# The last normalisation of a decoder layer: sums on VectorE, an earlier third token tile, a shorter Newton step, and a gain vector scaled beforehand

## The chip, the cores and the metric

The kernel runs on one core of one Trainium2 chip. The metric is device microseconds of that core for one execution, from the start of the program to its end. It is given as the median of several executions, and one further execution is taken by the hardware profiler.

## The reference

One layer of a hybrid decoder, on x of 1 x 512 x 1024 in float32, everything in float32:

```
u = rms_norm(x, norm_mix_g)
z = u @ w_in                        # q, k, v of attention; q, k, v, gates of the mLSTM; branch gates
A = block-sparse causal attention (8 heads x 64, rotary, blocks of 256)
B = chunkwise mLSTM (4 heads x 128, running-max stabiliser)
h = x + (sigmoid(gA) * (A @ w_proj_a) + sigmoid(gB) * (B @ w_proj_b)) @ w_out
u = rms_norm(h, norm_ffn_g)
g, up = split(u @ w_gate_up)        # 2 x 2816 columns
h = h + (silu(g) * up) @ w_down
return rms_norm(h, norm_final_g)

def rms_norm(x, g):
    return x * rsqrt(mean(x * x, axis=-1) + 1e-6) * g
```

The change concerns the last line: for each of the 512 tokens the sum of squares of its 1024 values of h, a reciprocal square root, and the product with it and with the gain vector `norm_final_g`.

## The kernel before

**Precision.** A float32 matmul is done as three TensorE products of float32r parts: each operand is split into a high part (`act_` with Copy on ScalarE, recorded at L155) and a low part, operand minus high part (VectorE, L168 in the helper `split_hl`, L847 in `gc_prep` for the weights of gate and up). One operand split thus always goes ScalarE first, then VectorE, then TensorE.

**The feed-forward part.** It is most of the program's second half. It runs through a list `ITEMS`: chunks "gc" of gate and up, single tiles "gu" of what is left of them, and chunks "ds" of the down projection. Each item is one level of Strassen's scheme: seven products named W11, S1, S2, W12, S3, S4 and W22. For each product of the first chunk, weights are loaded as `raw`, copied to w on ScalarE, and subtracted to a low w on VectorE (L847); sums of weights are made in DRAM by accumulating DMAs, `ws`. The other operand, `bq`, comes from the mixer's output and is split in the same way (ScalarE L155, VectorE L168) while the first products run already. TensorE's products of the chunk are L872, L873 and L874; their results are evacuated as `ga`, `gx` and `gb` on ScalarE and added to later products on VectorE (`gx` at L908).

**The second norm** falls into the first chunk. The column sums of squares of h are split into `sqh` (ScalarE) and `sql` (VectorE), both are multiplied by a matrix of ones on TensorE (L349), and the reciprocal root is computed and sent by DMA through DRAM to a per-token layout, `rg`, which the scaling of `gx` (ScalarE, L160) reads.

**What sets the order.** The kernel is written against a scheduler that keeps a priority for each instruction. `plan()` gives every product of every item a planned time, and `at(key, w, off)` sets the priority of what follows to that time plus an offset. An instruction may be placed ahead of its planned time where the scheduler finds its engine free and its operands there; `tc.issue_after(i)` keeps one behind instruction i. What comes out is one fixed sequence for each engine, and each engine takes its sequence in order. DMAs are issued by SyncE (SP), GpSimd (POOL) and in one case ScalarE.

**The end.** `end_load` (L1327 to L1336), called after the last but one "gu" item, loads the two halves of the final gain vector, `g3[0]` and `g3[1]`, broadcast to 128 partitions (128 x 512 each, DMA of L1332 on SP), and later the residual h in eight tiles `hs[t][j]`: token tile t of 128 tokens, column half j of 512. The two g3 loads wait for no computed value; the scheduler puts them on SP in the middle of the program, during the first gate-and-up chunk. Nothing reads g3 until the end.

`ds_end` (L1185 to L1325) is the last down chunk together with the final norm. Its matmuls are `ds_prod` (L1117 to L1119) and `last` (L1235 to L1237). Behind them, per token tile t and half j:

- `add_` (L1201, VectorE): h += product * factor of the second norm;
- `square` (ScalarE): squares of a half, with their sum as a second output;
- `rstd` (L1213 to L1217): VectorE adds the first sum and the epsilon to z, ScalarE takes Ln(e + z) and Exp(-0.5 * ...), e being the last sum, and VectorE forms v = e + z;
- `newton` (L327 to L335): one Newton step on that root r in three VectorE instructions, t = r*r, t = -0.5*t*v, t = (t + 1.5)*r;
- `apply` (L1221 to L1224): one half as h * factor * g on VectorE, the other, which `times_g` (L1227) has multiplied by g before, as h * factor on ScalarE, and then two stores on SP (for the fourth tile one of them on ScalarE).

The fourth token tile (t = 3) is last. Its half j = 1 is done in two column halves of 256 (`lo`, `hi`), so that the very last addition and square are half as wide. The third tile's `apply(2, ...)` is pinned behind that last addition.

Of the kernel before, what the change touches and what calls it, by code (L numbers as in the profile page):

```python
# [11 lines left out]
AF = mybir.ActivationFunctionType  # L12
ALU = mybir.AluOpType
# [4 lines left out]
D = 1024  # L18
# [5 lines left out]
EPS = 1e-6  # L24
# [67 lines left out]
def hybrid_layer_kernel(ctx: ExitStack, tc, xT, wall, wgc, wgu, wds, wdl, g3v, vecs, wgates, consts, rope, out):  # L92
    nc = tc.nc
    V, A, T = nc.vector, nc.scalar, nc.tensor
# [11 lines left out]
    def nm(p="t"):  # L106
        cnt[0] += 1
        return f"{p}{cnt[0]}"

    def slot(dt=F32, name="a"):  # L110
        return act.tile([P, S], dt, name=nm(name), tag="A")
# [8 lines left out]
    def blk2(dt=F32, name="b", raw=False):  # L120
        return blk(dt, name, raw).rearrange("p (x c) -> p x c", x=2)
# [18 lines left out]
    raw_ins = lambda i: getattr(i, "ins", i)  # L140

    def table(set_id):
        if ph["set"] == set_id:
            return
        with ExitStack() as es:
            for i in ph["ins"]:
                es.enter_context(tc.issue_after(i))
            ld = A.add_instruction(
                mybir.InstLoadActFuncSet(name=nc.get_next_instruction_name(), act_func_set_id=set_id)
            )  # L150
        ph.update(set=set_id, load=raw_ins(ld), ins=[])

    def act_(out_, in_, func, **kw):
        if func not in SETS:
            return A.activation(out_, in_, func, **kw)  # L155
        table(SETS[func])
        if ph["manual"]:
            return A.activation(out_, in_, func, **kw)
        with tc.issue_after(ph["load"]):
            i = A.activation(out_, in_, func, **kw)  # L160
        ph["ins"].append(raw_ins(i))
        return i
# [66 lines left out]
    for k in range(KT):  # L229
        for j in (0, 2) if k == 0 else (0,):  # L230
            c = slice(j * P, (j + 2) * P if k == 0 else S)
# [51 lines left out]
    for k in range(KT):  # L283
        if k < 4:
            t = blk2(F32R, "u", raw=k < 2)
# [5 lines left out]
        c = slice(0, P * len(halves[0]))  # L291
# [10 lines left out]
        for js in halves:  # L302
            if js[0]:
                c = slice(2 * P, S)
# [14 lines left out]
    for i in range(4):  # L319
        z = zqk["qk"[i // 2], i % 2] = slot(name="z")  # L320
# [8 lines left out]
    def newton(r, v, new):  # L329

        t = new()
        V.tensor_tensor(t, r, r, op=ALU.mult)
        V.scalar_tensor_tensor(t, t, -0.5, v, op0=ALU.mult, op1=ALU.mult)
        V.scalar_tensor_tensor(t, t, 1.5, r, op0=ALU.add, op1=ALU.mult)
        return t  # L335
# [467 lines left out]
    def at(key, w, off=0):  # L803
        t = clock["at"][key, w] + off
        tc.cur_priority = clock["base"] + (t if t > 0 else t // PRE)
# [379 lines left out]
    def ds_end():  # L1185


        n = NG - 1
        key = ("ds", n)
        w = sw.pop(key)["w"]  # L1190
        r, nr = ([st[x][:, t : t + 1] for t in range(4)] for x in ("rc", "nrc"))
        two = range(2)
        g3, hs = st["h"]
        ss = {}
        U = 1360
        v_ = lambda: small([P, 1], "v1")

        def add_(t, j, ps, c, d=slice(0, S)):

            h = hs[t][j][:, d]  # L1200
            return V.scalar_tensor_tensor(h, ps[:, d], c, h, op0=ALU.mult, op1=ALU.add)  # L1201

        def square(t, j, d=slice(0, S)):
            s = v_()
            act_(slot(name="sq")[:, d], hs[t][j][:, d], AF.Square, scale=D**-0.5, accum_out=s)
            ss.setdefault(t, []).append(s)

        def rstd(t, w_, o):

            at(key, w_, o - 600)  # L1210
            *s, e = ss[t]
            z, v, q = v_(), v_(), v_()
            i = V.tensor_scalar(z, s[0], s[-1] if len(s) > 1 else 0.0, EPS, op0=ALU.add, op1=ALU.add)  # L1213
            at(key, w_, o)
            act_(q, e, AF.Ln, bias=z)
            V.tensor_tensor(v, e, z, op=ALU.add)
            return q, v, (i, act_(q, q, AF.Exp, scale=-0.5))  # L1217

        def apply(t, q, j):

            V.scalar_tensor_tensor(hs[t][j], hs[t][j], q, g3[j], op0=ALU.mult, op1=ALU.mult)  # L1221
            act_(hs[t][1 - j], hs[t][1 - j], AF.Copy, scale=q)
            for e in (j, 1 - j):
                (nc.scalar if t == 3 and e != j else nc.sync).dma_start(out[t][:, e * S : e * S + S], hs[t][e])  # L1224

        def times_g(t, j):
            V.tensor_tensor(hs[t][j], hs[t][j], g3[j], op=ALU.mult)  # L1227

        def last(ps, t, j, first=False, d=slice(0, S)):

            q, c = slice(t * P, (t + 1) * P), slice(j * S + d.start, j * S + d.stop)
            for k in range(LK):
                (ah, al), (wh, wl) = hid[k], DL[k]
                g = dict(skip_group_check=not first)
                T.matmul(ps[:, d], ah[:, q], wh[:, c], start=first and k == 0, stop=False, **g)  # L1235
                T.matmul(ps[:, d], ah[:, q], wl[:, c], start=False, stop=False, **g)
                T.matmul(ps[:, d], al[:, q], wh[:, c], start=False, stop=k == LK - 1, **g)  # L1237

        qs = []
        X, Z = [mmb() for t in two], [sb() for t in two]  # L1240
        for t in two:
            at(key, "W11", U * t)
            ds_prod(X[t], w["W11"], n, 0, t, first=True)
            at(key, "S2", U * t)
            add_(t, 0, X[t], nr[t])
        for t in two:
            at(key, "S1", U * t)
            ds_prod(Z[t], w["S1"], n, 1, t, first=True)
        for t in two:
            at(key, "S2", U * t)  # L1250
            ds_prod(X[t], w["S2"], n, 4, t)
            at(key, "W12", U * t)
            add_(t + 2, 0, X[t], nr[t + 2])
        for t in two:
            at(key, "W12", 2 * U * t)
            y = accb()
            last(y, t, 0, first=True)
            ds_prod(y, w["W12"], n, 2, t)
            at(key, "W12", 2 * U * (t + 1) + D_OFF)
            add_(t, 0, y, r[t])  # L1260
            square(t, 0)
        for t in two:
            at(key, "S3", U * t)
            ds_prod(X[t], w["S3"], n, 5, t)
            at(key, "S3", U * t + D_OFF)
            add_(t + 2, 1, X[t], r[t + 2])
        for t in two:
            at(key, "W22", U * t - 1000)
            add_(t + 2, 1, Z[t], r[t + 2])
        at(key, "LAST")  # L1270
        y = accb()
        last(y, 2, 1, first=True)
        at(key, "W22", 2000)
        add_(2, 1, y, nr[2])
        square(2, 1)
        for t in two:
            at(key, "W22", 2 * U * t)
            ds_prod(X[t], w["W22"], n, 6, t)
            last(X[t], t, 1)
            at(key, "W22", 2 * U * t + 1000)  # L1280
            times_g(t, 0)
            at(key, "W22", 2 * U * (t + 1) + 200)
            add_(t, 1, X[t], r[t])
            square(t, 1)
            q, v, _ = rstd(t, "W22", 2 * U * (t + 1) + 2000)
            qs.append(newton(q, v, v_))
            if t == 0:
                apply(0, qs[0], 1)
        at(key, "S4")
        ds_prod(Z[0], w["S4"], n, 3, 0)  # L1290
        last(Z[0], 2, 0)
        at(key, "S4", 1000)
        times_g(2, 1)
        at(key, "S4", 2 * U + 200)
        add_(2, 0, Z[0], nr[2])
        square(2, 0)
        q, v, i = rstd(2, "S4", 2 * U + 1000)
        qs.append(newton(q, v, v_))
        at(key, "S4", 2 * U + 800)
        with tc.issue_after(raw_ins(i[1])):  # L1300
            apply(1, qs[1], 1)
        y = accb()
        lo, hi = slice(0, HS), slice(HS, S)
        at(key, "S4", 2 * U)
        last(y, 3, 1, first=True, d=lo)
        at(key, "S4", 3 * U)
        add_(3, 1, y, nr[3], lo)
        square(3, 1, lo)
        at(key, "S4", 5 * U // 2)
        ds_prod(Z[1], w["S4"], n, 3, 1)  # L1310
        last(Z[1], 3, 0)
        at(key, "S4", 9 * U // 2 + 200)
        add_(3, 0, Z[1], nr[3])
        square(3, 0)
        at(key, "S4", 9 * U // 2)
        last(y, 3, 1, first=True, d=hi)
        at(key, "S4", 5 * U + 200)
        i = add_(3, 1, y, nr[3], hi)
        square(3, 1, hi)
        with tc.issue_after(raw_ins(i)):  # L1320
            apply(2, qs[2], 0)
        q, v, i = rstd(3, "S4", 5 * U + 800)
        with tc.issue_after(raw_ins(i[0])):
            times_g(3, 0)
        apply(3, newton(q, v, v_), 1)  # L1325

    def end_load():  # L1327

# [405 lines left out]
    while n < len(steps) or qa or qb:  # L1734
        if qa and (len(qa) >= LA or n >= len(steps)):
            kind, h, b, r = qa.pop(0)
            qb.append((kind, h, b, moba_b(h, b, r) if kind == "a" else r, n))
        if n < len(steps):
# [3 lines left out]
            r, second = moba_a(h, b) if kind == "a" else ml_a(h, b)  # L1742
# [23 lines left out]
        while qb and (qb[0][4] <= n - LC):  # L1766
            kind, h, b, r, _ = qb.pop(0)
# [120 lines left out]
```

## Time and profile before

| | before |
|---|---|
| median of three executions | 720.25 us (719.82 to 720.83) |
| profiled execution, own time | 719.12 us |
| its span, from first to last recorded work | 717.3 us |
| mean granted TensorE clock | 0.998 of full speed |
| instructions | 9566 |
| DMA | 152.70 MB, mean 213 GB/s |
| chain that ended last, by engine | PE 84%, DVE 7%, ACT 5%, DMA 2% |

Engines are named as in the profile: PE is TensorE's matmul, PEld its weight load, DVE VectorE, ACT ScalarE, POOL GpSimd, SP SyncE; SPq and POOLq are the DMA issues of those two. A row of the timeline gives start and busy time in us, the engine, the line, the operation, the output and the operands by the program's names, and the tile's shape; in square brackets stands how long the engine was idle before it and what ended that. A row of the table of DMAs ends with the KB of one transfer and the median time from issue to landing. A row of the windows gives the stretch, its length, the busy time of PE, PEld, DVE, ACT and POOL (with the number of instructions), the granted clock, the mean busy share of the 16 DMA engines, and GB/s.

### The profile page before, as it was taken

The numbers are of one execution on the slowest core, as the hardware profiler recorded it, in microseconds if no ns is written. First come the engines' busy times: TensorE is split into PE (matmuls) and PEld (weight loads), VectorE is DVE, ScalarE is ACT, GpSimd is POOL, SyncE is SP. The second block draws the span as 40 slices with busy tenths as digits, with TensorE's granted clock in tenths as the row PEclk, the third lists the DMA queues.
The fourth block names the chain that finished last, engine by engine and source line by source line (L and its number), as shares of the span: only waits on it lengthen the run. The fifth ranks groups of instructions, "written<-read, shape, count | busy, mean of one in ns | idle before, by whom it ended". The sixth has DMA issues, their size and how long they took to land.

```text
span 717.3 us, 9566 instructions
## 1 busy us (share of the span) xinstructions
PE 707.3 (99%) x3318; PEld 588.4 (82%) x3318; DVE 601.4 (84%) x982; ACT 428.9 (60%) x706; POOL 69.9 (10%) x97
## 2 busy tenths in 40 slices
PE   9999999999999999999999999999999999999995
PEld 6888788888888888888888888888888888888974
DVE  6899886898987588666699869898899799798996
ACT  7634778669774346732354845566765665665655
POOL 0013010000001000000020110011002004003000
PEclk9999999999999999999999999999999999999999
DMA  9668683625158998988889866579569649969703
GB/s 331 283 211 238 200 230 119 201 90 191 60 184 220 278 268 247 273 255 230 224 270 237 252 224 197 214 185 297 192 196 273 220 134 222 312 162 275 203 1 118
DMA packets 47008, 152.70 MB, mean 213 GB/s; under 512 B 5852, under 2 KB 6244, under 8 KB 42480
## 3 DMA queue, kind: packets, MB, share of 16 engines
q1 hardware_dynamic: 36880, 117.39, 47.7%
q0 software_dynamic: 9792, 34.14, 22.9%
q8 instruction: 26, 0.43, 0.2%
q10 hardware_dynamic: 288, 0.56, 0.2%
q14 instruction: 22, 0.18, 0.1%
HBM read 130.01 MB, written 53.52 MB: 256 GB/s over the span
## 4 chain that ended last, share of the span: by engine, by line
PE 84%; DVE 7%; ACT 5%; DMA 2%; issue 1%; POOL 0%; ACTq 0%; DVEq 0%; POOLq 0%
PE mm L208 10%; PE mm L209 10%; PE mm L210 10%; PE mm L872 5%; PE mm L873 5%; PE mm L874 5%; PE s L873 2%; PE s L874 2%; PE s L872 2%; PE mm L1118 2%; PE mm L1119 2%; PE mm L1117 2%; PE mm L491 2%; PE mm L308 2%; PE mm L493 2%; PE mm L492 2%
## 5 line engine op out<-in xcount | busy, mean ns | idle before, releaser
L155 ACT ACTIVATE w<-raw 128x1024 fp32r<-128x1024 f32 (+2 forms) x107 | 108.1, 1023 | 49.1 <-PE mm L873 14.7
L155 ACT ACTIVATE wh<-raw 128x1024 fp32r<-128x1024 f32 x56 | 59.1, 1056 | 73.0 <-PE mm L209 70.7
L847 DVE TENSOR_TENSOR w<-raw,w 128x1024 fp32r<-128x1024 f32 x70 | 84.1, 1219 | 15.7 <-ACT w L155 15.6
L168 DVE TENSOR_TENSOR wl<-raw,wh 128x1024 fp32r<-128x1024 f32 x56 | 68.2, 1219 | 10.5 <-ACT wh L155 10.0
L872 PE MATMUL mm<-w,bq 128*128 128x512 f32 x160 | 62.4, 390 | 0.0
L874 PE MATMUL mm<-w,bq 128*128 128x512 f32 x160 | 62.3, 389 | 0.0
L873 PE MATMUL mm<-w,bq 128*128 128x512 f32 x160 | 62.2, 389 | 0.0
L208 PE MATMUL mm<-u,wh 128*128 128x512 f32 x128 | 50.6, 395 | 0.2 <-ACT ob L155 0.2
L210 PE MATMUL mm<-u,wh 128*128 128x512 f32 x128 | 50.1, 391 | 0.0
L209 PE MATMUL mm<-u,wl 128*128 128x512 f32 x128 | 49.9, 390 | 0.0
L210 PE MATMUL mm<-ul,wh 128*128 128x512 f32 x128 | 49.8, 389 | 0.0
L208 PE MATMUL mm<-uh,wh 128*128 128x512 f32 x128 | 49.8, 389 | 0.0
L209 PE MATMUL mm<-uh,wl 128*128 128x512 f32 x128 | 49.8, 389 | 0.0
L872 PEld LDWEIGHTS mm<-w,bq 128*128 128x128 f32 x160 | 30.0, 188 | 6.7 <-ACT gs L160 0.5
L873 PEld LDWEIGHTS mm<-w,bq 128*128 128x128 f32 x160 | 30.1, 188 | 6.2
L874 PEld LDWEIGHTS mm<-w,bq 128*128 128x128 f32 x160 | 30.0, 188 | 6.2
L1027 DVE TENSOR_TENSOR w<-raw,w 128x1024 fp32r<-128x1024 f32 x25 | 30.2, 1216 | 2.0 <-ACT w L155 1.0
L1117 PE MATMUL mm<-w,ac 128*128 128x512 f32 x80 | 31.3, 392 | 0.0
L1118 PE MATMUL mm<-w,ac 128*128 128x512 f32 x80 | 31.1, 389 | 0.0
L1119 PE MATMUL mm<-w,ac 128*128 128x512 f32 x80 | 31.1, 389 | 0.0
L872 PE MATMUL s<-w,bq 128*128 128x512 f32 x80 | 31.1, 389 | 0.0
L873 PE MATMUL s<-w,bq 128*128 128x512 f32 x80 | 31.1, 389 | 0.0
(439 smaller groups left out, 1942.0 us busy)
## 6 DMA issues: line engine op xcount, KB each, us to landing
raw<-in_wall_dram SPq DMA_DIRECT2D x56, 512.0 KB, 5.5
raw<-in_wgc_dram SPq DMA_DIRECT2D x30, 512.0 KB, 6.1
raw<-ws SPq DMA_DIRECT2D x30, 512.0 KB, 5.9
ws<-in_wgc_dram SPq DMA_DIRECT2D x10, 1024.0 KB, 6.5
ws<-in_wgc_dram POOLq DMA_DIRECT2D x10, 1024.0 KB, 10.1
raw<-in_wds_dram SPq DMA_DIRECT2D x15, 512.0 KB, 6.0
ws<-in_wds_dram SPq DMA_DIRECT2D x10, 512.0 KB, 7.9
ws<-in_wds_dram POOLq DMA_DIRECT2D x10, 512.0 KB, 7.0
```

The source lines that it names most:

```text
L155: return A.activation(out_, in_, func, **kw)
L168: V.tensor_tensor(l, src, f(h), op=ALU.subtract)
L208: st["mm"] = T.matmul(ps, wh[:, c], rh[j], start=start and j == 0, stop=False)
L209: T.matmul(ps, wl[:, c], rh[j], start=False, stop=False)
L210: T.matmul(ps, wh[:, c], rl[j], start=False, stop=stop and j == n - 1)
L847: V.tensor_tensor(l, t, f(h), op=ALU.subtract)
L872: st["mm"] = T.matmul(ps[t], bh, wh[:, d], start=first and k == 0, stop=False, skip_group_check=not first)
L873: T.matmul(ps[t], bh, wl[:, d], start=False, stop=False, skip_group_check=not first)
L874: T.matmul(ps[t], bl, wh[:, d], start=False, stop=k == 3, skip_group_check=not first)
L1117: T.matmul(ps, bh, wh[:, d], start=first and k == 0, stop=False, skip_group_check=not first)
L1118: T.matmul(ps, bh, wl[:, d], start=False, stop=False, skip_group_check=not first)
L1119: T.matmul(ps, bl, wh[:, d], start=False, stop=k == 1, skip_group_check=not first)
```

## The change

It has four parts, all in `ds_end`.

1. Both halves of the gain vector are multiplied by -0.5 on ScalarE, in place, at the planned time of the chunk's first product.
2. `rstd` is split into `start` (z, Ln, Exp) and `finish`. With -0.5 in the gain, a Newton step takes two VectorE instructions instead of three: c = q*v*q and r = (c - 3)*q, which is -2 times the value of before. v = e + z stands in `finish`.
3. The third tile's Newton step and `apply(2, ...)` are chained behind `apply(1, ...)` and ahead of the addition of tile 3, half 0, where `apply(2, ...)` stood behind the last addition before. `apply(1, ...)` is now pinned behind the first quarter's addition of tile 3 as well.
4. The last squares (128 x 256 of tile 3) are summed on VectorE by one instruction that multiplies, scales by 1/1024 and sums, starting from z3 (the first square's sum plus the epsilon), where ScalarE squared before; the last square of half 0 enters as the bias of Ln. `times_g(3, 0)` is pinned behind v instead of z.

```diff
@@ ds_end
         g3, hs = st["h"]
+        at(key, "W11")
+        for g in g3:
+            act_(g, g, AF.Copy, scale=-0.5)
...
+            z, q = v_(), v_()
+            V.tensor_scalar(z, s[0], s[-1] if len(s) > 1 else 0.0, EPS, op0=ALU.add, op1=ALU.add)
             at(key, w_, o)
+            cs[t] = q, e, z
             act_(q, e, AF.Ln, bias=z)
+            return act_(q, q, AF.Exp, scale=-0.5)
+
+        def finish(t):
+
+            q, e, z = cs[t]
+            v, c, r = v_(), v_(), v_()
             V.tensor_tensor(v, e, z, op=ALU.add)
-            return q, v, (i, act_(q, q, AF.Exp, scale=-0.5))
+            V.scalar_tensor_tensor(c, q, v, q, op0=ALU.mult, op1=ALU.mult)
+            return r, V.scalar_tensor_tensor(r, c, -3.0, q, op0=ALU.add, op1=ALU.mult)
...
-        q, v, i = rstd(2, "S4", 2 * U + 1000)
-        qs.append(newton(q, v, v_))
-        at(key, "S4", 2 * U + 800)
-        with tc.issue_after(raw_ins(i[1])):
-            apply(1, qs[1], 1)
+        j2 = start(2, "S4", 2 * U + 1000)
...
         at(key, "S4", 3 * U)
-        add_(3, 1, y, nr[3], lo)
+        i = add_(3, 1, y, nr[3], lo)
         square(3, 1, lo)
+        at(key, "S4", 2 * U + 900)
+        with tc.issue_after(raw_ins(i)), tc.issue_after(raw_ins(j2)):
+            i = apply(1, qs[1], 1)
+        with tc.issue_after(raw_ins(i)):
+            rr = finish(2)
+        qs.append(rr[0])
+        with tc.issue_after(raw_ins(rr[1])):
+            i = apply(2, qs[2], 0)
+        z3 = v_()
+        with tc.issue_after(raw_ins(i)):
+            V.tensor_scalar(z3, ss[3][0], EPS, None, op0=ALU.add)
...
-        add_(3, 0, Z[1], nr[3])
+        with tc.issue_after(raw_ins(i)):
+            add_(3, 0, Z[1], nr[3])
         square(3, 0)
         at(key, "S4", 9 * U // 2)
         last(y, 3, 1, first=True, d=hi)
         at(key, "S4", 5 * U + 200)
-        i = add_(3, 1, y, nr[3], hi)
-        square(3, 1, hi)
+        add_(3, 1, y, nr[3], hi)
+        e = v_()
+        i = V.tensor_tensor_reduce(
+            slot(name="sq")[:, hi], hs[3][1][:, hi], hs[3][1][:, hi], 1.0 / D, z3, op0=ALU.mult, op1=ALU.add, accum_out=e,
+        )
+        at(key, "S4", 5 * U + 800)
+        q, v, c, r = (v_() for _ in range(4))
+        act_(q, e, AF.Ln, bias=ss[3][1])
+        act_(q, q, AF.Exp, scale=-0.5)
+        i = V.tensor_tensor(v, e, ss[3][1], op=ALU.add)
         with tc.issue_after(raw_ins(i)):
-            apply(2, qs[2], 0)
-        q, v, i = rstd(3, "S4", 5 * U + 800)
-        with tc.issue_after(raw_ins(i[0])):
-            times_g(3, 0)
-        apply(3, newton(q, v, v_), 1)
+            i = times_g(3, 0)
+        with tc.issue_after(raw_ins(i)):
+            V.scalar_tensor_tensor(c, q, v, q, op0=ALU.mult, op1=ALU.mult)
+        V.scalar_tensor_tensor(r, c, -3.0, q, op0=ALU.add, op1=ALU.mult)
+        apply(3, r, 1)
```

The sequences of TensorE, GpSimd and SyncE are the same before and after, but for the order of the two stores of tiles 0 and 2. ScalarE has one instruction more, VectorE two fewer.

Where the two scalings of g3 stand is not where the code stands. The first is in ScalarE's sequence in the middle of the program, in the first gate-and-up chunk. In the names, the trailing numbers are buffers: g31317 is g3[0], w a weight's high part made from raw, bq the other operand's high part made from v1.

```order
 L155 ACTIVATE bq763_3689<-ut779_3781 128x512
 L155 ACTIVATE w795_3819<-raw767_3699 128x1024
+L155 ACTIVATE g31317_6274<-g31317_6274 128x512
 L155 ACTIVATE bq773_3737<-v1816_3889 128x512
 L155 ACTIVATE w797_3823<-raw768_3700 128x1024
```

One instruction is new, between the copy of a weight and the split of an operand; around it nothing is moved. The second, g31318 for g3[1], stands some twenty instructions further on in the same sequence, among the copies of weights.

```order
 L148 ACT_TABLE_LOAD
 L155 ACTIVATE w811_3853<-raw785_3797 128x1024
+L155 ACTIVATE g31318_6275<-g31318_6275 128x512
 L155 ACTIVATE w813_3857<-raw786_3798 128x1024
 L155 ACTIVATE w829_3925<-raw819_3905 128x1024
```

Again one row is added and none is moved. The last place is VectorE's end. Before, from the third tile's Newton step (L332 to L334) on; h11323 is tile 2 half 0, h11325 and h11326 are tile 3 halves 0 and 1, and the 128x1 tiles v1... are the sums and factors of one value per token:

```order
L332 TENSOR_TENSOR v11406_6701<-v11405_6696 128x1
L333 SCALAR_TENSOR_TENSOR v11406_6701<-v11406_6701,v11404_6695 128x1
L334 SCALAR_TENSOR_TENSOR v11406_6701<-v11406_6701,v11405_6696 128x1
L1201 SCALAR_TENSOR_TENSOR h11325_6282<-s1379_6514,nrc2_4096,h11325_6282 128x512
L1201 SCALAR_TENSOR_TENSOR h11326_6283<-acc1407_6709,nrc2_4096,h11326_6283 128x256
L1221 SCALAR_TENSOR_TENSOR h11323_6280<-h11323_6280,v11406_6701,g31317_6274 128x512
L1213 TENSOR_SCALAR v11414_6750<-v11408_6717,v11410_6733 128x1
L1227 TENSOR_TENSOR h11325_6282<-h11325_6282,g31317_6274 128x512
```

And the same stretch in the changed kernel, where L1235 and L1236 are the Newton step, L1240 is the third tile's scaling, L1204 are the additions and L1347 is the sum of squares:

```order
L1235 SCALAR_TENSOR_TENSOR v11411_6717<-v11406_6697,v11410_6716 128x1
L1236 SCALAR_TENSOR_TENSOR v11412_6718<-v11411_6717,v11406_6697 128x1
L1240 SCALAR_TENSOR_TENSOR h11323_6280<-h11323_6280,v11412_6718,g31317_6274 128x512
L1334 TENSOR_SCALAR v11413_6726<-v11408_6709 128x1
L1204 SCALAR_TENSOR_TENSOR h11325_6282<-s1379_6516,nrc2_4096,h11325_6282 128x512
L1204 SCALAR_TENSOR_TENSOR h11326_6283<-acc1407_6701,nrc2_4096,h11326_6283 128x256
L1347 ISA sq1417_6752,v11416_6751<-h11326_6283,v11413_6726 128x256
L1347 ISA v11416_6751 128x1
L1354 TENSOR_TENSOR v11419_6755<-v11416_6751,v11414_6741 128x1
L1247 TENSOR_TENSOR h11325_6282<-h11325_6282,g31317_6274 128x512
L1358 SCALAR_TENSOR_TENSOR v11420_6756<-v11418_6754,v11419_6755 128x1
L1359 SCALAR_TENSOR_TENSOR v11421_6757<-v11420_6756,v11418_6754 128x1
```

The third tile's scaling (h11323) has moved from behind both additions to ahead of them, the Newton step has one row fewer, and behind the second addition stands the sum of squares where before the third tile's scaling stood. On ScalarE the third tile's Exp now stands behind the half-wide square of tile 3 (sq1409), and the very last square has gone:

```order
L160 ACTIVATE v11406_6697<-v11403_6693,v11405_6696 128x1
L155 ACTIVATE sq1409_6710,v11408_6709<-h11326_6283 128x256
L160 ACTIVATE v11406_6697<-v11406_6697 128x1
L155 ACTIVATE h11321_6278<-h11321_6278,v11402_6675 128x512
L155 ACTIVATE h11324_6281<-h11324_6281,v11412_6718 128x512
L155 ACTIVATE sq1415_6742,v11414_6741<-h11325_6282 128x512
```

Before, these rows were Ln and Exp of tile 2 next to each other, then the scaling of h11321, the half-wide square, the scaling of h11324 and the full square.

More of the change, by code (lines that the diff above doesn't have):

```diff
@@ L1210, in rstd, with start @@
             at(key, w_, o - 600)
+            i = start(t, w_, o)
+            return finish(t)[0], i
+        cs = {}
+        def start(t, w_, o):
+            at(key, w_, o - 600)
             *s, e = ss[t]
-            z, v, q = v_(), v_(), v_()
-            i = V.tensor_scalar(z, s[0], s[-1] if len(s) > 1 else 0.0, EPS, op0=ALU.add, op1=ALU.add)
+            z, q = v_(), v_()
+            V.tensor_scalar(z, s[0], s[-1] if len(s) > 1 else 0.0, EPS, op0=ALU.add, op1=ALU.add)
             at(key, w_, o)
+            cs[t] = q, e, z
             act_(q, e, AF.Ln, bias=z)
+            return act_(q, q, AF.Exp, scale=-0.5)
+        def finish(t):
+            q, e, z = cs[t]
+            v, c, r = v_(), v_(), v_()
             V.tensor_tensor(v, e, z, op=ALU.add)
-            return q, v, (i, act_(q, q, AF.Exp, scale=-0.5))
+            V.scalar_tensor_tensor(c, q, v, q, op0=ALU.mult, op1=ALU.mult)
+            return r, V.scalar_tensor_tensor(r, c, -3.0, q, op0=ALU.add, op1=ALU.mult)
         def apply(t, q, j):
-            V.scalar_tensor_tensor(hs[t][j], hs[t][j], q, g3[j], op0=ALU.mult, op1=ALU.mult)
+            i = V.scalar_tensor_tensor(hs[t][j], hs[t][j], q, g3[j], op0=ALU.mult, op1=ALU.mult)
             act_(hs[t][1 - j], hs[t][1 - j], AF.Copy, scale=q)
@@ L1224, in apply @@
                 (nc.scalar if t == 3 and e != j else nc.sync).dma_start(out[t][:, e * S : e * S + S], hs[t][e])
+            return i
         def times_g(t, j):
-            V.tensor_tensor(hs[t][j], hs[t][j], g3[j], op=ALU.mult)
+            return V.tensor_tensor(hs[t][j], hs[t][j], g3[j], op=ALU.mult)
         def last(ps, t, j, first=False, d=slice(0, S)):
@@ L1284, in ds_end @@
             square(t, 1)
-            q, v, _ = rstd(t, "W22", 2 * U * (t + 1) + 2000)
-            qs.append(newton(q, v, v_))
+            qs.append(rstd(t, "W22", 2 * U * (t + 1) + 2000)[0])
             if t == 0:
@@ L1296, in ds_end @@
         square(2, 0)
-        q, v, i = rstd(2, "S4", 2 * U + 1000)
-        qs.append(newton(q, v, v_))
-        at(key, "S4", 2 * U + 800)
-        with tc.issue_after(raw_ins(i[1])):
-            apply(1, qs[1], 1)
+        j2 = start(2, "S4", 2 * U + 1000)
         y = accb()
```

## The prediction

> **What bounds the kernel now.** First the page: which engine is full.
>
> ```profile
> PE 707.3 (99%) x3318; PEld 588.4 (82%) x3318; DVE 601.4 (84%) x982; ACT 428.9 (60%) x706; POOL 69.9 (10%) x97
> ```
>
> TensorE works through 99% of the span. Two things follow. Up to the last matmul an edit can save nearly nothing, but whatever makes TensorE wait is paid in full; behind the last matmul a short tail is open to be shortened. So two places were read: the chain of waits at the end, and, because the order shows two new ScalarE instructions in mid-program, the timeline of every engine around them. The end first, as the chain that ended last tells it (start, length, what):
>
> ```profile
> 708.68 0.24 PE s L1237
> 708.95 1.19 DVE h L1201 x2
> 710.14 0.66 DVE h L1221
> ...
> 711.59 0.16 DVE v L332
> 711.78 0.17 DVE v L333
> 711.97 0.17 DVE v L334
> 712.16 0.75 DVE h L1221
> ```
>
> From the last full-width product (708.9) to the end of the last scaling (712.91) are 4.0 us on VectorE: two additions, the scaling of the third tile, the Newton step, the scaling of the fourth. That is all the part named "end of the kernel" can shorten.
>
> Now the middle, where the first gain vector is loaded, with ScalarE's rows from the timeline, the load's time to landing and the stretch's shares:
>
> ```profile
> 388.66 0.33 SPq L1332 DMA_DIRECT2D g<-in_g3v_dram  x1
> ...
> g<-in_g3v_dram SPq DMA_DIRECT2D x1, 256.0 KB, 9.3
> ...
> 389.36 1.06 ACT L155 ACTIVATE w<-raw 128x1024 fp32r<-128x1024 f32 x1
> 393.23 0.63 ACT L155 ACTIVATE bq<-v 128x512 fp32r<-128x512 f32 x1 [2.81 <-DVE v L702]
> ...
> 395.91 1.07 ACT L155 ACTIVATE ga<-mm 128x512 f32<-128x512 f32 x2
> ...
> 388.00:398.00 10.00, 10.00 (x45) 8.26 (x44) 10.00 (x17) 5.69 (x9) 0.50 (x1) 1.00 1.00 247
> ```
>
> The load of g3[0] is issued at 388.66 and lands 9.3 later, at 398.0: the DMA engines are 100% busy there. Before the change nothing reads it until the last stage, so this cost nothing. The last row is the stretch 388 to 398: busy microseconds of PE, PEld, DVE, ACT and POOL, granted clock, DMA share. TensorE and VectorE are both 100% busy there.
>
> **The change part by part.** *The scaling of g3 by -0.5 on ScalarE.* By the order it stands directly behind the weight copy w of 389.36 and ahead of the copy bq of 393.23. The load is not moved: SyncE's order is unchanged, and the load waits for work that lies ahead of the new instruction. So ScalarE is free at 390.42, waits until 398.0, starts about 0.1 later, and can start bq 0.53 after that (two such instructions take 1.07 at 395.91), at 398.6 instead of 393.23. It ends at 399.2. Queued behind it are a weight copy, a square, the two evacuations ga and more weight copies; TensorE and VectorE wait for them:
>
> ```profile
> 394.25 0.68 DVE L168 TENSOR_TENSOR bq<-v,bq 128x512 fp32r<-128x512 f32 x1
> ...
> 403.68 2.34 DVE L847 TENSOR_TENSOR w<-raw,w 128x1024 fp32r<-128x1024 f32 x2
> 406.77 1.23 DVE L847 TENSOR_TENSOR w<-raw,w 128x1024 fp32r<-128x1024 f32 x1 [0.76 <-ACT w L155]
> 407.92 0.69 DVE L168 TENSOR_TENSOR sql<-sq,sqh 128x512 fp32r<-128x512 f32 x1
> ...
> 400.27 0.39 PE L872 MATMUL mm<-w,bq 128*128 128x512 f32 x1
> 407.80 0.50 PE L349 MATMUL s<-sqh,onesr 128*128 128x512 f32 x1
> 408.13 0.40 PE L872 MATMUL acc<-w,bq 128*128 128x512 f32 x1
> 408.37 0.39 PE L873 MATMUL acc<-w,bq 128*128 128x512 f32 x1
> ...
> 408.83 0.40 PE L349 MATMUL s<-sql,onesr 128*128 128x512 f32 x1
> ```
>
> VectorE's bq of 394.25 reads ScalarE's bq, so it starts at 399.25, 5.0 late. From it to the end of the two w of 403.68 VectorE has no gap; then comes one of 0.8 (the 0.76 of the row and 0.09 of overlap), which swallows part: sql, at 407.92, comes 5.0 - 0.8 = 4.2 late, and ends at 412.8. TensorE's matmul on sql (408.83) now starts 0.2 after sql ends, so it becomes **4.0 late**. On the way the same 4.0 build up: ga ends at about 401.2 (bq, then w, sq, ga), so the product of 400.27 starts 1.0 late; the next w from VectorE adds 0.6, sqh 1.3, sql the remaining 1.1. Restarting after a stall costs 0.1 (407.80 to 408.13 is 0.33, where neighbours stand 0.23 apart). Against it a stall that exists now disappears:
>
> ```profile
> 429.24 0.39 PE L874 MATMUL mm<-w,bq 128*128 128x512 f32 x1
> 429.68 0.50 PE L872 MATMUL mm<-w,bq 128*128 128x512 f32 x1
> ...
> 425.82 1.34 ACT L160 ACTIVATE gx<-gx,rg 128x512 f32<-128x512 f32 x2 [4.84 <-DMA rg<-row]
> ```
>
> 0.44 instead of 0.23, and the restart, are 0.3 us. What it waits for hangs on the norm computed behind sql and on a DMA, and will be 3 to 4 late, no later than TensorE itself. Sum for this part: 4.0 + 0.1 - 0.3 = **+3.8 us**. Nothing gives it back: later TensorE pauses only for results made from its own products.
>
> The bounds of that wait are the times to landing of the loads issued next to it:
>
> ```profile
> ws<-in_wgc_dram POOLq DMA_DIRECT2D x1, 1024.0 KB, 10.1
> raw<-in_wgc_dram SPq DMA_DIRECT2D x1, 512.0 KB, 3.7
> ```
>
> With 3.7, g3[0] is there at 392.4, bq is not delayed and the part costs 0; with 10.1 it costs 0.8 more, 4.6. I take 9.3: it is this very load, and nothing ahead of it changes. Between the ends each microsecond of landing is a microsecond of time once it lands after 394.0.
>
> That a waiting ScalarE instruction holds all behind it, this trace shows at 425.82: ScalarE idles 4.84 us for rg, and the weight copies that stand next in its order run only afterwards. [...]
>
> *The scaling of g3[1].* It stands behind a weight copy that ends near 413.5 and ahead of that of 414.48:
>
> ```profile
> 406.43 0.58 SPq L1332 DMA_DIRECT2D g<-in_g3v_dram  x1
> ...
> g<-in_g3v_dram SPq DMA_DIRECT2D x1, 256.0 KB, 10.0
> ...
> 414.48 1.06 ACT L155 ACTIVATE w<-raw 128x1024 fp32r<-128x1024 f32 x1 [1.01 <-PE mm L873]
> ...
> 416.90 1.28 DVE L908 TENSOR_TENSOR gx<-mm,gx 128x512 f32<-128x512 f32 x2
> ...
> 422.67 0.39 PE L872 MATMUL mm<-w,bq 128*128 128x512 f32 x1
> ```
>
> Its load waits in SyncE's queue behind one that VectorE's late w releases, so it is issued 5 later and lands near 421.5. The copy of 414.48 then runs at 422.2, VectorE's w behind it, then gx, until 425.1. TensorE needs gx for the matmul of 422.67, itself 4.1 late, 426.8. Cover 1.7 us; cost 0.
>
> *The end.* The third tile's Exp now stands behind the half-width square in ScalarE's order, and its Newton step and scaling ahead of the addition of 708.95:
>
> ```profile
> 707.59 0.20 ACT L160 ACTIVATE v<-v 128x1 f32<-128x1 f32 x1
> ...
> 708.32 0.40 ACT L155 ACTIVATE sq<-h 128x256 f32<-128x256 f32 x1
> ...
> 708.72 0.71 ACT L155 ACTIVATE h<-h,v 128x512 f32<-128x512 f32 x1
> ...
> L1511 DVE CUSTOM_DVE_ANT_0 ms<-s,mask 128x256 f32<-128x256 f32 x8 | 3.3, 417 | 0.0
> ...
> 710.83 2.45 SPq L1224 DMA_DIRECT2D out_dram<-h  x2
> ```
>
> In before's clock: such a square holds the next instruction 0.4; about 0.1 of it overlaps Ln, so Exp ends at 708.1 instead of 707.8. Two dependent Newton operations at 0.19 (711.78 to 711.97), then the scaling: 708.5 to 709.1, then a [128,1] operation of 0.07. The addition starts at 709.2, 0.26 late; the half addition ends at 710.35, and its sum of squares, 0.42 by the row of the same custom form, at 710.8. Ln, Exp: 710.9 to 711.45, 0.1 sooner than now. VectorE meanwhile multiplies by g until 711.57, so the two Newton operations start there and the scaling at 711.95 instead of 712.16: **-0.2 us**. The third tile's stores leave 1.4 us earlier; now they are issued by 710.83 and do not meet the last pair either way. Bounds: -0.45 if Exp comes as early as now, +0.1 if it comes 0.3 later. The shorter Newton steps of the first two tiles lie beside matmuls: 0; uncovered, 0.3.
>
> **The sum.** The profiled execution took 719.12 (span 717.3 and 1.8 around it): 719.12 + 3.8 - 0.2 = 722.7. It lies 1.13 under the median of 720.25; by the median 723.85, about 723.9.
>
> **Rivals.**
> (a) *The other side: ScalarE does not wait in vain.* If g3[0] lands by 394.0, 5.3 us after its issue, only the end counts: 720.0, between -0.45 and +0.1. For it: the neighbouring 3.7. Against it: a DMA share of 1.00 and two neighbours at 9.3 and 10.1. 8%.
> (b) *A smaller stall*, landing 6 to 7.5 us after issue, so 0.7 to 2.2 late: 720.7 to 722.2. 6%.
> (c) *The clock falls on top.* Between 409.4 and 412.8 TensorE would stand still for 2.4 of 3.4 us. The granted clock falls in this trace only after the last matmul (0.58 over the second row is half clock from about 714.5 on, some 5 us behind it), and the pause of 0.2 us at 429.68 leaves it at 1.00:
>
> ```profile
> 422.00:430.00 8.00, 7.95 (x35) 6.29 (x34) 4.55 (x8) 4.18 (x6) 0.00 (x0) 1.00 0.15 53
> 714.00:717.30 3.30, 0.00 (x0) 0.00 (x0) 0.00 (x0) 0.00 (x0) 0.00 (x0) 0.58 0.35 136
> ```
>
> At half clock for 3.4 us TensorE would do half the work: 1.7 more, 725.6. 6%. [...]
> (d) *The second scaling reaches TensorE*, if its load takes over 11.7: up to 1.5 more, 725.4. 4%.
>
> **How the numbers follow.** Forecast as worked out 76%, between 722 and 725. About 0.2%, 1.44 us, is what a measurement can tell from no change. Slower by more: 76 + 6 + 4 and about half of (b), 89%; within: 9%; faster: 2%, since the whole end can give 0.45. The range takes in the wait from 7.3 to 10.1, the end's bounds and most of (c) and (d): 721.8 to 725.4.
>
> **What would show it.** Right: a g row on ScalarE near 398 with 7 to 8 us idle ahead, ended by the DMA g; TensorE gaps near 401, 404, 410 and 412 of 1.0, 0.6, 1.3 and 1.1; the last matmul 3.8 later; the tail from it to the last scaling shorter by 0.2. Wrong: g lands before 394, or VectorE catches up more than 0.8 ahead of sql, or TensorE's lag shrinks after 430.

## The result and the profile after

| | before | after |
|---|---|---|
| median | 720.03 us (719.43 to 720.83, 6 runs) | 725.34 us (723.32 to 726.75, 6 runs) |
| profiled execution, own time | 719.12 us | 726.54 us |
| its span | 717.3 us | 724.7 us |
| last matmul's start to the span's end | 7.96 us | 7.95 us |

The ratio is 1.0071 with a 95% interval of 1.0057 to 1.0086: the changed kernel is slower by 5.3 us; 3.6 were forecast (3.8 - 0.2). Its times also scatter more widely, over 3.4 us instead of 1.4.

The first line of the page of after: TensorE is busy 2.7 us longer than before (710.0 against 707.3) for the same matmuls, some of which ran at half clock; the rest of the loss is waiting.

```profile
PE 710.0 (98%) x3318; PEld 590.1 (81%) x3318; DVE 602.0 (83%) x980; ACT 429.3 (59%) x706; POOL 69.8 (10%) x97
```

ScalarE's timeline of after, in the middle of the program (start, length, engine, line, operation; in brackets idle time before it and what ended that):

```profile
390.48 1.04 ACT L155 ACTIVATE w<-raw 128x1024 fp32r<-128x1024 f32 x1
401.67 0.63 ACT L155 ACTIVATE g<-g 128x512 f32<-128x512 f32 x1 [10.14 <-DMA g<-in_g3v_dram]
402.20 0.61 ACT L155 ACTIVATE bq<-v 128x512 fp32r<-128x512 f32 x1
...
423.39 0.63 ACT L155 ACTIVATE g<-g 128x512 f32<-128x512 f32 x1 [2.70 <-DMA g<-in_g3v_dram]
```

ScalarE stands still for 10.14 us for g3[0], and bq, which ran at 393.23 before, follows at 402.20. The chain that ended last now runs through that load (start, length, what):

```profile
389.97 11.62 DMA g<-in_g3v_dram
...
402.85 0.69 DVE bq L168
...
415.67 0.70 DVE sql L168
...
416.42 0.50 PE s L349
```

It is the chain of the forecast: load, ScalarE's bq, VectorE's bq, VectorE without a gap of note up to sql, TensorE's matmul on sql. TensorE's timeline shows how its lag builds up, and the windows (stretch, length, busy PE, PEld, DVE, ACT, POOL, granted clock, DMA share, GB/s) show the clock:

```profile
404.81 0.50 PE L872 MATMUL mm<-w,bq 128*128 128x512 f32 x1 [3.31 <-ACT ga L155]
405.15 0.40 PE L873 MATMUL mm<-w,bq 128*128 128x512 f32 x1
...
408.10 0.63 PE L873 MATMUL mm<-w,bq 128*128 128x512 f32 x1
...
416.42 0.50 PE L349 MATMUL s<-sql,onesr 128*128 128x512 f32 x1 [1.15 <-DVE sql L168]
```

```profile
400.00:404.80 4.80, 1.50 (x7) 0.93 (x5) 1.95 (x3) 3.13 (x6) 0.78 (x1) 1.00 0.79 236
404.80:409.80 5.00, 4.99 (x15) 3.95 (x16) 5.00 (x9) 4.56 (x8) 0.00 (x0) 0.66 0.66 100
```

One wait of 3.3 us, then products at half clock (0.63 us each instead of 0.39, the granted clock 0.50 from 407 to 409), then a wait of 1.15. The matmul on sql starts at 416.42 instead of 408.83. Of these 7.59 us, 1.08 belong to no part of the change: already the products behind the first load of the program are that much later (the other kernels stand at -0.1 to 1.0 there). That leaves **6.51 us**, of which 6.35 are left at the last matmul (716.77 against 709.34, less 1.08).

The end of after, from the chain; the last matmul starts at 716.77:

```profile
715.97 0.75 DVE h L1240
716.73 0.06 DVE v L1334
716.79 1.06 DVE h L1204 x2
...
717.88 0.48 DVE sq L1347
...
718.47 0.16 DVE v L1354
718.63 0.06 DVE h L1247
718.69 0.46 issue
719.15 0.22 DVE v L1358
719.38 0.02 issue
719.40 0.17 DVE v L1359
719.57 0.03 issue
719.60 0.75 DVE h L1240
```

The order is the forecast one, but the last scaling starts 2.83 us behind the start of the last matmul; in before it was 2.82 (712.16 against 709.34). The end gives nothing.

So the profiled execution is 7.42 longer: 1.08 from the start of the program, 6.35 from the middle, 0.0 from the end.

### The profile page after: what moved, and what is told of

Read it like the earlier page. It is cut to its first block, busy times and chain, and to the rows that moved or that the text cites. A ratio compares the mean times of both kernels' runs of the same rounds, so it can differ in the third digit from the quotient of the medians.

```text
span 724.7 us, 9560 instructions
## 1 busy us (share of the span) xinstructions
PE 710.0 (98%) x3318; PEld 590.1 (81%) x3318; DVE 602.0 (83%) x980; ACT 429.3 (59%) x706; POOL 69.8 (10%) x97
## 4 chain that ended last, share of the span: by engine, by line
PE 79%; DVE 11%; ACT 5%; DMA 3%; issue 2%; ACTq 0%; DVEq 0%; SPq 0%
PE mm L208 9%; PE mm L209 9%; PE mm L210 9%; PE mm L872 5%; PE mm L873 5%; PE mm L874 5%; PE s L872 2%; PE s L873 2%; PE s L874 2%; PE mm L1118 2%; PE mm L1119 2%; PE mm L1117 2%; PE mm L308 2%; DMA g<-in_g3v_dram 2%; PE mm L491 2%
## 5 line engine op out<-in xcount | busy, mean ns | idle before, releaser
L168 DVE TENSOR_TENSOR wl<-raw,wh 128x1024 fp32r<-128x1024 f32 x56 | 68.3, 1221 | 10.7 <-ACT wh L155 10.4
L872 PE MATMUL mm<-w,bq 128*128 128x512 f32 x160 | 63.1, 394 | 3.3 <-ACT ga L155 3.3
L873 PE MATMUL mm<-w,bq 128*128 128x512 f32 x160 | 62.9, 393 | 0.0
L874 PE MATMUL mm<-w,bq 128*128 128x512 f32 x160 | 62.9, 393 | 0.0
L872 PEld LDWEIGHTS mm<-w,bq 128*128 128x128 f32 x160 | 30.4, 190 | 10.1 <-ACT ga L155 3.7
```

Source lines behind the costliest of these rows:

```text
L168: V.tensor_tensor(l, src, f(h), op=ALU.subtract)
L872: st["mm"] = T.matmul(ps[t], bh, wh[:, d], start=first and k == 0, stop=False, skip_group_check=not first)
L873: T.matmul(ps[t], bh, wl[:, d], start=False, stop=False, skip_group_check=not first)
L874: T.matmul(ps[t], bl, wh[:, d], start=False, stop=k == 3, skip_group_check=not first)
```

## The experiments

**Is it the wait, and the wait alone?** Four kernels take the two scalings apart from the rest. `e1_late` pins both behind an instruction that runs when the loads have long landed:

```diff
@@ gc_run
-            act_(s, X[t], AF.Silu, scale=rg[:, t : t + 1])
+            i = act_(s, X[t], AF.Silu, scale=rg[:, t : t + 1])
+            st.setdefault("pin", raw_ins(i))
@@ ds_end
         at(key, "W11")
         for g in g3:
-            act_(g, g, AF.Copy, scale=-0.5)
+            with tc.issue_after(st["pin"]):
+                act_(g, g, AF.Copy, scale=-0.5)
```

> The changed kernel with both scalings of g3 pinned behind the first evacuation gs of the first chunk (before: 429.7), some 13 us behind the second load's landing; nothing else differs. Theory A (all of the loss is ScalarE's wait for the loads): the mid-program stalls are gone, the time is that of before plus what the end gives, 0.0 by the profile of after: 719.8 to 720.3 beside a before of 720.0. Rival R1 (the loss, or a part, lies in the end or in the instructions themselves): it stays above 722.

`e2_scale_only` is the reverse, the kernel before with only the two instructions (factor 1.0):

```diff
         g3, hs = st["h"]
+        at(key, "W11")
+        for g in g3:
+            act_(g, g, AF.Copy, scale=1.0)
```

> The kernel before, with nothing added but the two copies of g3 on ScalarE, scaled by 1.0, at the place they have in the changed kernel. Theory A: as slow as the changed kernel, 723.3 to 726.8 by the landing of the first load, with g idle 9 to 11 us on ScalarE and TensorE's matmul on sql late by the landing minus 394.0 on the clock of before. Rival R1: 720 to 721.

`e4_second_early` leaves only the second scaling at its place in mid-program; `e5_first_early` has the two halves exchanged and leaves only the first:

```diff
-        for g in g3:
-            act_(g, g, AF.Copy, scale=-0.5)
+        with tc.issue_after(st["pin"]):
+            act_(g3[0], g3[0], AF.Copy, scale=-0.5)
+        act_(g3[1], g3[1], AF.Copy, scale=-0.5)
```

> The changed kernel with only the first scaling, of g3[0], pinned late as in e1_late; that of g3[1] stays where it is. Theory A: ScalarE still waits for the second load, to about 416.5 on the clock of before, the weight copy of 414.48 comes 2 to 3 us late, and the slack of 5 us ahead of TensorE's next use of gx swallows it: 719.8 to 720.5. Rival R3 (the second wait reaches TensorE too): 721 to 722.5.

> The changed kernel with only the scaling of g3[0] at its place in mid-program; that of g3[1] is pinned late. Theory A (the first wait alone makes the loss): TensorE's matmul on sql is late by the time from the issue of the first load to its landing, less 5.3 us (10.3 to 11.8 us in the runs so far, so 5.0 to 6.5 late), and the time is 723.3 to 726.8. If the clock falls to half behind the matmul on sql, as in e2_scale_only, 1.6 to 1.7 us come on top; if ahead of it, as in the changed kernel, nothing. Rival R3 (a good part comes from the second wait): under 722.5.

| | median (lowest to highest) | before beside it | ratio, 95% interval |
|---|---|---|---|
| e1_late | 719.56 (719.18 to 720.88) | 719.57 | 1.0003, 0.9994 to 1.0012 |
| e2_scale_only | 725.77 (725.33 to 726.67) | 719.57 | 1.0089, 1.0076 to 1.0102 |
| e4_second_early | 719.83 (719.18 to 723.89) | 719.57 | 1.0011, 1.0000 to 1.0021 |
| e5_first_early | 724.48 (723.67 to 726.69) | 719.74 | 1.0076, 1.0061 to 1.0091 |

The loss is there with the first scaling at its place and gone without it; the rest of the change neither adds to it nor takes from it, to within the interval of e1 (0.9 us at most). The second scaling waits too (3.44 us in the profile of e4) and TensorE does not feel it, as forecast; whether the one run at 723.89 is a case of it cannot be told, since it has no trace. Its mean granted clock was 0.994, where the other eleven show 0.996 to 0.998.

**How much does each microsecond of landing cost?** The forecast said: the lag at sql is the landing minus 394.0. Five kernels with the first wait in place test this, since the load lands differently each time. All times are on the clock of before, that is, less the shift that TensorE's matmuls already have ahead of the place:

| | landing after issue | landed at | minus 394.0 | measured lag at sql |
|---|---|---|---|---|
| after | 11.62 | 400.51 | 6.51 | 6.51 |
| e2_scale_only | 10.27 | 398.84 | 4.84 | 4.84 |
| e3_fill | 10.81 | 398.79 | 4.79 | 4.79 |
| e5_first_early | 10.98 | 399.53 | 5.53 | 5.53 |
| e6_first_early_fill | 12.26 | 402.23 | 8.23 | 8.23 |

The rule holds to 0.01 us, whether products ran at half clock ahead of sql or not. In the kernels without the first wait the same load took 10.7 to 11.8 us (e1, e4, e7, e8, e9), and the lag at sql is 0.01 at most.

**Does the half clock come on top?** `e3_fill` adds matmuls that nothing reads, to keep TensorE busy while it waits for ga:

```diff
+        if c == 0:
+            Y = [accb() for _ in two]
+            at(key, "S2", -1)
+            for _ in range(12):
+                T.matmul(Y[0], onesr, bq[(0, 0)].rearrange("p x c -> p (x c)")[:, 0:S], start=True, stop=True)
         product(X, "S2", 4)
```

> The changed kernel with 12 matmuls of 128x512 (2.7 us) added that nothing reads, around the place where TensorE waits for ga, so that it does not stand still there. Theory A with a clock that costs nothing (the half clock of after, 4.9 us long, only takes from the later wait for sql): the granted clock stays 1.00, the wait for ga shrinks to under 1 us, the wait for sql grows from 1.3 to about 3, and the time is that of the changed kernel, 723.3 to 726.8 by the landing. Rival R2 (the clock falls on top, as rival (c) of the prediction has it): 1.7 less than the changed kernel, about 723.6 in the median, with the wait for sql still at 1.3.

It came out at 730.98 us (ratio 1.0157, 1.0144 to 1.0170), outside both expectations, because it changed more than it was meant to. All but one of the added matmuls landed among the products behind the wait, and the scheduler moved the second scaling ahead of the norm's root r. ScalarE and TensorE of e3:

```profile
412.02 0.62 ACT L155 ACTIVATE sqh<-sq 128x512 fp32r<-128x512 f32 x1
422.16 0.63 ACT L155 ACTIVATE g<-g 128x512 f32<-128x512 f32 x1 [9.53 <-DMA g<-in_g3v_dram]
422.70 1.04 ACT L155 ACTIVATE w<-raw 128x1024 fp32r<-128x1024 f32 x1
423.65 0.67 ACT L160 ACTIVATE r<-s,epsc 128x512 f32<-128x512 f32 x1
```

```profile
431.62 0.77 PE L872 MATMUL mm<-w,bq 128*128 128x512 f32 x1 [3.47 <-DVE gx L914]
432.18 0.63 PE L873 MATMUL mm<-w,bq 128*128 128x512 f32 x1
```

This is rival (d) at full size: a few rows further up, the second wait is 9.5 us, holds everything behind it, and costs TensorE a stall of 3.5 and a stretch at half clock (0.63 us a product; the mean granted clock is 0.57 from 431 to 435). On the clock's share it decides nothing. `e6_first_early_fill` puts the matmuls in one row ahead of the product, without the second scaling:

```diff
-            at(key, "S2", -1)
-            for _ in range(12):
-                T.matmul(Y[0], onesr, bq[(0, 0)].rearrange("p x c -> p (x c)")[:, 0:S], start=True, stop=True)
+            at(key, "S2", -1400)
+            for k in range(12):
+                T.matmul(Y[0], onesr, bq[(0, 0)].rearrange("p x c -> p (x c)")[:, 0:S], start=k == 0, stop=k == 11)
```

> e5_first_early with 12 matmuls of 128x512 (2.7 us) that nothing reads, in one row ahead of the product that waits for ga; SyncE's load of g3[1] stands ahead of one transfer for a sum of weights instead of behind it. Theory A: they lie in the wait, the wait for ga shrinks to under 1 us, TensorE's matmul on sql is late by the landing less 5.3 us as without them, within 0.3, and no half clock follows anywhere, so the time is that of e5_first_early or up to 1.7 below it. Rival R4 (filling costs, or the clock falls nevertheless): the lag at sql exceeds that sum by 1 to 2.7, or products stand 0.43 apart behind it.

726.98 us (723.47 to 728.04), ratio 1.0094, 1.0076 to 1.0112, 2.5 above e5. By the letter the expectation missed: it counted from the issue, and here the load was issued 1.3 us later than in before on the same clock and landed 12.3 after it, so 2.24 us of the wait for ga were left and the lag is 8.23. Counted from the landing, as in the table, the lag is right. One of its rows of windows, and the DMA row:

```profile
406.00:418.00 12.00, 9.64 (x38) 7.00 (x39) 12.00 (x16) 9.81 (x15) 2.68 (x4) 1.00 0.57 147
```

```profile
g<-in_g3v_dram SPq DMA_DIRECT2D x1, 256.0 KB, 12.3
```

The clock stays at 1.00, and no half-speed product follows. Its six executions have a mean granted clock of 0.996 to 0.998, while three of e5's six have 0.994. That speaks for the added matmuls, but it is not shown that they kept the clock up: the wait that was left, 2.24 us, is nearly the 2.33 of e5, behind which it fell. The issue hangs on a residual load ahead of it, which took 8.3 us there; why both loads took longer is open. SyncE and GpSimd issue a few transfers in another order in this kernel, and that was not tried by itself.

What the half clock costs is read from two profiles side by side. In after (above; the mean clock of 0.66 over 5.0 us is 3.4 us at 0.50, not the 4.9 of the expectation of e3) it falls behind the wait for ga, ahead of sql: the slow products use up time that TensorE would have waited for sql anyway, and the lag at sql is 6.51 as the rule has it. In e5 it is the same (lag 5.53):

```profile
402.70:407.00 4.30, 4.30 (x12) 3.40 (x13) 4.30 (x8) 3.87 (x7) 0.00 (x0) 0.60 0.71 118
```

In e2 it falls behind sql:

```profile
411.22 0.50 PE L349 MATMUL s<-sqh,onesr 128*128 128x512 f32 x1 [0.75 <-ACT sqh L155]
411.56 0.40 PE L872 MATMUL acc<-w,bq 128*128 128x512 f32 x1
...
413.65 0.50 PE L349 MATMUL s<-sql,onesr 128*128 128x512 f32 x1 [1.23 <-DVE sql L168]
413.99 0.56 PE L872 MATMUL acc<-w,bq 128*128 128x512 f32 x1
414.34 0.63 PE L873 MATMUL acc<-w,bq 128*128 128x512 f32 x1
414.77 0.63 PE L874 MATMUL acc<-w,bq 128*128 128x512 f32 x1
...
417.33 0.46 PE L874 MATMUL acc<-w,bq 128*128 128x512 f32 x1
```

Here nothing is late behind it any more, and it is paid: the lag grows from 4.84 at sql to 6.53 at 418.1, of which 0.1 is the restart and 1.6 the clock.

That a fall ahead of sql costs nothing is read from two profiles. Of the six executions of after, the three longest (725.88 to 726.75) have a mean granted clock of 0.994 or 0.995, the three shortest (723.32 to 724.79) 0.997 or 0.998; before's executions show 0.996 to 0.998. In e5 the times do not part in this way: 724.37, 724.41 and 726.69 at 0.994, and 723.67, 724.56 and 726.30 at 0.996 to 0.998. Only one execution of each was traced, so it stays open whether the clock has a share in the scatter of after, or falls where the load is late anyway.

**Does it help to bring the load forward instead?** `e10_load_earlier` is e5 with a third buffer for the tiles that g3 shares with the mixer's residual loads:

```diff
-    NX = 2
+    NX = 3
```

> e5_first_early with three buffers instead of two for the tiles that g3 and the residual loads share: SyncE issues the load of g3[0] some 7 us earlier, at 381 on the clock of before, and the scheduler places its scaling four rows earlier on ScalarE, ahead of the square of 385.71. Theory A (only the time by which the landing lies behind the point at which ScalarE would go on counts): it lands 6 to 12 us after issue, at 387.5 to 393; behind it stand a square, a copy of 0.6 and one of 1.0 ahead of the copy of 393.23, so a landing by 390.6 costs nothing and each us beyond is one; 719.6 to 721.5. Rival R8 (the scaling in mid-program costs what it costs wherever the load stands): 723.3 or more.

720.42 us (719.58 to 721.19), ratio 1.0008, 0.9999 to 1.0017, as theory A has it. ScalarE of e10, and the load's row:

```profile
385.16 0.61 ACT L155 ACTIVATE bq<-v 128x512 fp32r<-128x512 f32 x1
388.45 0.63 ACT L155 ACTIVATE g<-g 128x512 f32<-128x512 f32 x1 [2.68 <-DMA g<-in_g3v_dram]
...
394.37 0.63 ACT L155 ACTIVATE bq<-v 128x512 fp32r<-128x512 f32 x1 [3.29 <-DVE v L702]
```

```profile
g<-in_g3v_dram SPq DMA_DIRECT2D x1, 256.0 KB, 6.8
```

The same instruction still waits in mid-program, 2.68 us, but the copy bq of 394.37 waits for VectorE's v, as in before: the wait has cover. Load and scaling both came earlier in this kernel, the scaling by three rows of ScalarE's timeline (a square, a copy bq and a weight copy now stand behind it; the expectation says four); the two were not tried apart.

**What does the end give?** `e7_newton` has the end of before with the Newton step in two operations and the scalings pinned late:

```diff
-            qs.append(newton(q, v, v_))
+            qs.append(newton2(q, v))
...
+        def newton2(q, v):
+            c, r = v_(), v_()
+            V.scalar_tensor_tensor(c, q, v, q, op0=ALU.mult, op1=ALU.mult)
+            V.scalar_tensor_tensor(r, c, -3.0, q, op0=ALU.add, op1=ALU.mult)
```

> The kernel before with both scalings of g3 by -0.5 pinned late as in e1_late, and the Newton step in two operations; the end is otherwise that of before. The tail from the start of the last matmul to the end of the span is 7.94 to 7.96 in before and e2_scale_only, which have the three operations. Theory A: one operation of 0.16 to 0.19 less on the chain, tail 7.75 to 7.80. Rival R5 (something else ends last there): 7.94.

The tail is 7.93, the time 719.91 (ratio 1.0002, 0.9993 to 1.0011). Its chain:

```profile
712.69 0.16 DVE v L1221
...
712.95 0.23 DVE v L1227
713.18 0.02 issue
713.20 0.17 DVE v L1228
713.37 0.02 issue
713.39 0.75 DVE h L1233
```

From the start of v to the scaling it takes 0.70 us; before it was 0.72 (711.44 to 712.16) with one operation more. Before, the first of the three operations, r*r, needed only Exp's result and started 0.15 behind v. Now the first operation needs v itself and starts 0.26 behind it, and takes 0.23 instead of 0.16: the operation that was saved is spent on waiting for v.

`e8_exp_first`, with the scalings pinned late as in e1, lets Exp of the third tile run ahead of the half-wide square, which stood in its way in after:

```diff
         i = add_(3, 1, y, nr[3], lo)
-        square(3, 1, lo)
+        with tc.issue_after(raw_ins(j2)):
+            square(3, 1, lo)
```

> e1_late with the half-wide square of tile 3 pinned behind the third tile's Exp on ScalarE, so that Exp does not wait for the square. Theory A (the third tile's factor comes 0.4 late for that square, and so the additions of tile 3 start 0.3 late): additions follow the matmul at once, tail 7.6 to 7.7 instead of 7.87 to 7.97; the time is then 719.2 to 719.6 beside a before of 719.6, at the edge of what five rounds tell. Rival R6 (the additions wait for something else, or the gain is lost behind them): tail 7.9.

The tail grew to 8.31 (719.80 us, ratio 1.0006, 0.9997 to 1.0014). VectorE's row:

```profile
708.78 0.22 DVE L1237 SCALAR_TENSOR_TENSOR v<-v,v 128x1 f32<-128x1 f32 x1 [0.53 <-ACT h L155]
```

Exp was done at 708.13, but the first Newton operation waits for ScalarE's scaling h, which reads a 128x1 tile. There are six buffers for these tiles, and with the new order the operation takes over the one that h still reads. `e9_more_small` gives them two more, and moves the pin of the scalings to the second evacuation gs:

```diff
-    sm = ctx.enter_context(tc.tile_pool(name="sm", bufs=6))
+    sm = ctx.enter_context(tc.tile_pool(name="sm", bufs=8))
```

> e8_exp_first with eight buffers instead of six for the 128x1 tiles, and the scalings of g3 pinned behind the chunk's second evacuation gs instead of the first. In e8_exp_first the first Newton operation of the third tile stood still for 0.53 us until ScalarE's scaling of h11321 was done, which reads the 128x1 tile whose buffer it takes over. Theory A (that buffer alone cost it): the operation starts 0.05 behind Exp, the additions of tile 3 follow their matmul, tail 7.6 to 7.7, 0.3 below before and after; time 0.2 to 0.4 below before. Rival R7 (the two operations are late for another reason, or the gain is lost behind the additions): tail 7.9 or more.

The wait is gone, but the tail is 7.90, as R7 has it (719.69 us against 720.04, ratio 0.9994, 0.9985 to 1.0003, not to be told from no change):

```profile
708.61 0.23 DVE v L1238
...
709.06 0.75 DVE h L1243
...
709.88 1.06 DVE h L1207 x2
```

VectorE is at the scaling ahead of it, that of the second tile, until 708.35, v stands behind it, and the first Newton operation starts another 0.26 behind v. From there to the end of the additions VectorE has no gap, and the third tile's scaling of 0.7 us ahead of them is in the way whenever Exp ends.

## Why the prediction was right, and where its sizes were off

*The mechanism* held in every link: a ScalarE that waits for a load (10.14 us in after) and takes bq, next in its order, only then (402.20), VectorE behind it, sql as the point at which TensorE's lag is set, and 394.0 as the landing from which it costs. e1, e2, e4 and e5 show that this wait is the whole loss, and the table that the arithmetic (5.0 - 0.8 - 0.2) was right. The four small stalls of the forecast (1.0, 0.6, 1.3 and 1.1) are to be seen in e2, as 1.65, 0.35, 0.75 and 1.23 us of idle time; in after the first is 3.31, half clock follows, and one more, 1.15, is left.

*The size that was off is the landing.* The prediction took 9.3 us, as "this very load, and nothing ahead of it changes", and 10.1 as the upper end. In the ten other profiles in which the load stands at this place on SyncE (after and e1 to e9) it took 10.3 to 12.3 us; before's 9.35 is the shortest of all eleven. One profile is one draw, and the upper end was two microseconds short. That alone is 4.0 against 6.5 in the profiled pair, and since the lag follows the landing one to one, landings that differ by 2 us between runs would account for most of the scatter of after (3.4 us; only one of its runs was profiled, and a share of the clock is not excluded).

*That the time lies in the range is partly luck.* The median of 725.34 is 0.06 below the range's upper end, 725.4, and above the 722 to 725 that were given 76%; three of the six executions (725.88, 726.54 and 726.75) are above the range. The upper bounds of the landing and of the end alone make 719.12 + 4.6 + 0.1 + 1.13 = 724.95. The rest of the room had been left for rivals (c) and (d), and in the profiled execution neither of them added anything.

*The stall at 429.68* was to give back 0.3, its restart included. In after the lag against before falls there from 7.71 to 7.36 us, so 0.35 came back; 0.07 of it was lost again between 650 and 700.

*Rival (c)*, a half clock on top, was given 6% and a condition, a pause of 2.4 in 3.4 us around sqh and sql. The clock fell in all three profiles in which TensorE felt the first wait and no matmuls were added, so 6% was too little. No run had shown the 3.4 us of half clock that the rival reckons with; before shows half clock only from 714.5 to its end at 717.3. What came lasted as long: 3.4 us in each of the three, worked out from the mean clocks of 0.66 over 5.0 us (after), 0.61 over 4.4 (e2) and 0.60 over 4.3 (e5), with the 0.50 that after shows from 407 to 409. In e2 it fell where the rival has it, behind the waits for sqh and sql, and cost 1.6, near its 1.7. In after and e5 it fell sooner, behind the wait for ga, which the rival did not think of, and cost nothing, since sql set the lag anyway.

*The second scaling* cost nothing in after and e4, as forecast; e3 shows that this hung on its place in the order.

*The end*: forecast -0.2, measured 0.0. Against the last matmul, the additions start 0.08 later than worked out (716.71, which is 709.28 in before's clock, against 709.2). The sum of squares was priced with the 0.42 of an equal custom form; it takes 0.48, then its accumulator is read (0.08), and v starts 0.62 behind the additions' end where 0.45 was reckoned. VectorE's product with g, behind v, therefore ends 0.15 later, and the two Newton operations, which needed Exp only by 718.99, wait for it. What the two operations save is there (0.45 us from the first to the scaling against 0.58), and it is all used up; it is also 0.07 less than forecast, which had 0.38 from the first operation to the scaling (711.57 to 711.95).

## What to carry to other kernels

The instruction added to ScalarE cost what it waited for, less the slack of whatever stood behind it in the sequence: 6.51 us of lag for a wait of 10.14 in after, and no more than 0.17% of the time for one of 2.68 in e10. Look up where the scheduler has put it, not where the code stands, and pin it behind something that runs after its load. A landing time from one profile is one draw (here 9.35 to 12.3 us for the same load in eleven): where a result hangs on it one to one, take the range from all loads in the same stretch and leave room above. An operation saved in a chain of tiny dependent ones gave nothing where its successor depended on a later input than it did (e7: 0.70 us from v to the scaling with two operations, 0.72 with three): look at what the successor waits for before counting the saving.

## What had not been expected of the hardware

The clock fell without a long pause, and nearly the same pauses did not always have a fall behind them. In e2 waits of 0.75 and 1.23 us with four matmuls between them were followed by half clock, from 414.1 to 417.5 (0.63 us a product, a mean clock of 0.61 from 413.6 to 418.0); in e6 nearly the same two waits (0.73 before 415.24, 1.22 before 417.67) were not, nor was its wait of 2.24 us (the clock is 1.00 from 398 to 440), while in e5 one of 2.33 was (0.60 from 402.7 to 407.0). The prediction had given a fall behind two such waits 6%. What made the difference between e2 and e6 is not shown.

The load of 256 KB took 6.8 us when issued at 381.3 on the clock of before (e10), and 9.3 to 12.3 when issued at 388 to 390.
